# DRAM weight sums for two pairs per transfer and outside attention, factors of the last up pair in two parts, norm between the first up tiles, PSUM pools fixed per MLP

## Chip, cores and metric

One core of one Trainium2 chip. The metric is the device time of one execution in microseconds; the median of three runs of the kernel before is 1159.86 (1158.82 to 1163.74).

## What is computed

One step of a two-layer streaming encoder on 512 prompt frames and 64 sample frames, which the kernel treats together as T = 576 tokens, in halves of HT = 288. Model width 1024, hidden width of the MLP 4096, all in float32.

```python
x = x + pool_mixer(rmsnorm(x))                 # layer 0
x = x + mlp(rmsnorm(x), w_up[0], w_down[0])
x = x + sparse_attention(rmsnorm(x))           # layer 1: indexer scores, top-k, softmax on the chosen keys, w_o
x = x + mlp(rmsnorm(x), w_up[1], w_down[1])
y = rmsnorm(x)

def _mlp(h, w_up, w_down):
    u = jax.nn.relu(h @ w_up)
    return (u * u) @ w_down
```

## The kernel before

**Arithmetic.** Every weight and activation is split in a high and a low part (ACT casts the high part at L206, VectorE or, in the late part of attention, GpSimd subtracts for the low part at L207), and each product is three matmuls: high by high, high by low, low by high. With 128x128 weight blocks and 288 tokens in a matmul, TensorE has 8118 matmuls.

**The MLPs** run in four chunks of 1024 hidden units. A chunk has four up steps `up(c, q)`, each two tiles of 128 hidden units, and four down steps. Three forms of a step exist. A *plain* up step (L558) multiplies tile by tile. A *pair* (`DownPair`, L463, and `UpPair`, L475) is a 2x2 block product with seven multiplications in place of eight (Strassen's scheme in Winograd's form); it needs four sums of weight blocks, s1 to s4, and seven factors of the activations, among them four sums t1 to t4. Layer 0 has plain ups and 16 down pairs; its weight sums are made by GpSimd in SBUF (L267 to L272). Layer 1 has 12 up pairs (chunks 1 to 3), 12 down pairs (chunks 0 to 2), plain ups in chunk 0 and plain downs in chunk 3. The program order is: the ups of chunk c, then the first up of chunk c+1, then the downs of chunk c. The factors of a finished up step (squared ReLU times norm, sums, casts: L578 to L602) are needed by the first down pair of the chunk.

**Layer 1's weight sums are made in DRAM.** For each of the 24 pairs and each of s1 to s4 SyncE issues a copy of one 256 KB block into the DRAM tile `mixed` (L228), and GpSimd issues a DMA that accumulates another block on it (L222, `accum_op=add`). s2 builds on s1, s4 on s2. The generator `mixing()` (L209) yields 56 steps; `next(mixes)` drives it: one step in each up step of layer 0 and each up pair of layer 1, one in each down step, and one in each attention step from u = 18 on (L1358). The copies issued in layer 0's part are 61, in attention 35, in layer 1's MLP none. SyncE loads the finished sums in layer 1 as weights (`raw<-mixed`, L145).

**Queues.** SyncE's instruction stream is a single queue, in order: loads of MLP weights, copies into `mixed`, moves of q (L1282, L1286), cache_k loads (L1087), x from its copy in DRAM (L1397). ScalarE issues loads of w_o and w_in (L145) in its own stream, between its computations. GpSimd's stream holds the accumulates between its arithmetic. An instruction that waits holds all behind it in its stream. The order within a stream is set by a scheduler with a model of time (its table isn't part of the kernel), from the program order.

**PSUM** has eight banks. A phase opens pools (`stage`): at the start of an MLP six banks `po` and two `pf`; at the first pair this phase is closed and opened anew with two `seeds` and six `po` (layer 1), or `seeds`, four `po` and two `pd` (layer 0). The norm's sums and its spread over the partitions (L329 to L341) take banks from `po`, after the first two up tiles.

Of the kernel before, what the change touches and what calls it, by code (L numbers as in the profile page):

```python
# [16 lines left out]
P = 128  # L17
D = 1024
KT = D // P
# [30 lines left out]
def pool_dsa_kernel(ctx: ExitStack, tc: tile.TileContext, a, o):  # L50
# [56 lines left out]
    def f32(t):  # L107
        return t.bitcast(F32)
# [43 lines left out]
    mixed = dram.tile([P, 28, 4, 512], F32, name="mixed")  # L152
    pairs = {}
    for c in range(4):
        for q in range(PLAIN[1][c], 4):
            pairs["up", c, q] = len(pairs)
        if c < 3:
            for q in range(4):
                pairs["down", c, q] = len(pairs)

    def rows(kind, layer, c, q):

# [46 lines left out]

    def mixing():  # L210

        def parts(p):
            kind, c, q = order[p]
            (a11, a12), (a21, a22) = ([r[:, i * 512:(i + 1) * 512] for i in range(2)] for r in rows(kind, 1, c, q))
            s1, s2, s3, s4 = (mixed[:, p, i] for i in range(4))
            return {"s1": (s1, a21, a22), "s3": (s3, a21, a11), "s2": (s2, s1, a11), "s4": (s4, s2, a12)}

        order, copied = list(pairs), []
        for n in range(len(order) + 4):
            for step in (((n, "s1"), (n, "s3")), ((n - 1, "s2"), (n - 2, "s4"))):  # L220
                for dst, add in copied:
                    pool.dma_start(dst, add, accum_op=ALU.add)  # L222
                copied.clear()
                for p, name in step:
                    if 0 <= p < len(order):
                        dst, src, add = parts(p)[name]
                        with tc.issue_after(last_of["sync"].ins):
                            nc.sync.dma_start(dst, src)  # L228
                        copied.append((dst, add))
                yield  # L230

    mixes = mixing()

    def loaded():

        waiting, held = [], 0
        while jobs or waiting:
            while jobs and held < LOADS_AHEAD["more" in phase] and ("last" in phase or jobs[0][0] not in ("pair", "made")):
                kind, *srcs = jobs.pop(0)
                if kind == "made":  # L240
                    r1, r2 = rows(srcs[0], 1, *srcs[1:])
                    m = mixed[:, pairs[tuple(srcs)]].rearrange("p a b -> p (a b)")
                    srcs = [r1, m[:, :1024], m[:, 1024:], r2[:, 512:]]
# [57 lines left out]
    def project(pt, w, xs, between=iter(()), cols=((0, HT), (HT, HT))):  # L301

        n = len(xs)
        for k in range(n):
            next(between, None)
            wh, wl = at(w, k)
            for i, (wt, part) in enumerate(((wh, 0), (wh, 1), (wl, 0))):
                for h, (c, m) in enumerate(cols):
                    pe.matmul(  # L309
                        pt[h][:, :m] if isinstance(pt, tuple) else pt[:, h, :m], wt, xs[k][:, part, c:c + m],  # L310
                        start=(k == 0 and i == 0), stop=(k == n - 1 and i == 2),
                    )

    class Norm:
# [19 lines left out]
        def spread(self):  # L334
            diag = diagonals(self.r)
            self.rb = tmp("rb" + self.s, "rb", 1)
            for h in range(2):
                pb = psum1("rb")
                pe.matmul(pb[:, :HT], ones, diag[:, h * HT:(h + 1) * HT], start=True, stop=True)
                act.copy(self.rb[:, h * HT:(h + 1) * HT], pb[:, :HT])  # L340
            return self.rb  # L341
# [131 lines left out]
            dve.tensor_tensor(d, d, bank[:, :HT], ALU.add)  # L473

    class UpPair(Pair):  # L475
        def __init__(self, us, seeded, v):
            super().__init__(us, seeded, True)
            self.v = v
# [6 lines left out]
        def out(self, i, h, bank):  # L485
            d = self.v[:, 2 * i + h]
            if h:
                act.copy(d, bank[:, :HT])
            else:
                dve.tensor_tensor(d, self.e[:, i], bank[:, :HT], ALU.add)  # L490

    def mlp(layer, gi, strassen, order=range(KT), end=None):
        us = [[None] * KT for _ in range(4)]
# [64 lines left out]

        def up_plain(order):
            w = next_block()  # L560
            pt = [psum1("up", "pf" if "pf" in phase and not turn[0] else "po") for _ in range(2)]
            turn[0] += 1
            for n, k in enumerate(order):
                for i, (part, wt) in enumerate(((0, 0), (1, 0), (0, 1))):
                    for h in range(2):
                        pe.matmul(pt[h][:, :HT], w[:, wt, k * P:(k + 1) * P], moving(k, part, h),  # L566
                                  start=n == 0 and i == 0, stop=n == KT - 1 and i == 2)
            return pt
# [35 lines left out]
        def factors_by_tile(i, v, u):  # L604
# [41 lines left out]
        turn, banks = [0], []  # L646

        def seeded():
            if not banks:
                turn[0] = 0  # L650
                parts.close()
                parts.enter_context(stage(seeds=1, po=6) if layer else stage(seeds=1, pd=2, po=4))
                banks.extend(phase["seeds"].tile([P, 512], F32, tag=f"seed{i}", bufs=1, name=uid("seed")) for i in range(2))
            turn[0] += 1
            if turn[0] <= len(banks):
                pe.matmul(banks[turn[0] - 1][:, :HT], ones, bx0, start=True, stop=True, skip_group_check=True)
            return banks[(turn[0] - 1) % len(banks)]
# [1 line left out]
        bx0 = norm.s2[:, :HT]  # L659

        def up(c, q):
            if not layer or q >= PLAIN[layer][c]:
                next(mixes, None)
            if q >= PLAIN[layer][c]:
                v = new_v()
                pair = UpPair(bx, seeded(), v)
                pair.opening()
                pair.closing()
                activated(v)
                finished(c, q, v)  # L670
                return
            first = (c, q) == (0, 0)
            pts = []
            if not layer and not first and not late:
                v = new_v()
                for i in range(2):
                    pt = up_plain(range(KT))
                    for h in range(2):
                        dve.scalar_tensor_tensor(v[:, 2 * i + h], pt[h][:, :HT], 0.0, halves(norm.rb)[:, h], ALU.max, ALU.mult)
                    act.activation(v[:, 2 * i:2 * i + 2], v[:, 2 * i:2 * i + 2], AF.Square)  # L680
                    if (c, q) == (3, 3):
                        us[c][q] = us[c][q] or u_tile()
                        factors_by_tile(i, v, us[c][q])
                if us[c][q] is None or q == 0:
                    finished(c, q, v)
                return
            for i in range(2):
                pts.append(up_plain(order if first else range(KT)))
                if late:
                    norm.spread()  # L690
                    v = new_v()
                    activated(v, late.pop())
                    finished(c, 0, v)
                if not first:
                    with tc.issue_after(last_of["diag"].ins), tc.issue_after(last_of["rt"].ins):
                        next(mixed, None)
            if first:
                norm.stats()
                late.append(pts)
                return  # L700
            v = new_v()
            activated(v, pts)
            finished(c, q, v)

        late, mixed = [], mixing()
# [324 lines left out]
    def attention(parts):  # L1030
# [302 lines left out]
        def steps():  # L1333

            ranked = {0}
            for u in range(-4, total + 2):
# [178 lines left out]
```

## Time and profile before

| | us |
|---|---|
| median of three runs | 1159.86 |
| profiled execution | 1165.96 |
| its span | 1164.2 |
| pooling mixer | 0 to 43 |
| MLP of layer 0 | 43 to 441 |
| projections of attention and index scores | 441 to 606 |
| late attention (softmax, values, w_o) | 606 to 741 |
| MLP of layer 1 | 741 to 1093 |
| final norm and the last downs | 1093 to 1164 |

The stages' bounds are read from the timeline. In the views, `out<-in` names the tiles that an instruction writes and reads; `idle before <-X` in brackets is the time for which the engine had nothing to do ahead of it and what ended that. PE is TensorE, DVE VectorE, ACT ScalarE, POOL GpSimd, SP SyncE, and a `q` behind an engine's name (SPq, ACTq, POOLq) is its DMA issuing. In a row of the waits the numbers are microseconds in total, times, and the longest.

### The profile page before, as it was taken

To read this page: it belongs to the slowest core of one execution; us is meant where nothing else is said; L and a number is where in the kernel's file an instruction comes from. 1 tells how busy PE (TensorE), PEld (TensorE's weight loads), DVE (VectorE), ACT (ScalarE), POOL (GpSimd) and SP (SyncE) were. 2 spreads that over 40 slices of the span, in tenths; PEclk is the share of its full clock that TensorE was granted. 3 is DMA by queue.
4 is the path that set the end of the run, shared out by engine and by line. 5 is a ranking of instruction groups with operands and counts; after the bars stand their busy time and mean duration, and the time that the engine had idled before them with its cause. 6 is when DMAs were issued, how large, how long until landed. Compare 5 with 4: busy or idle time off the path is not lost.

```text
span 1164.2 us, 20675 instructions
## 1 busy us (share of the span) xinstructions
PE 1104.6 (95%) x8118; PEld 1086.0 (93%) x8118; DVE 808.9 (69%) x1438; ACT 555.6 (48%) x925; POOL 307.4 (26%) x275
## 2 busy tenths in 40 slices
PE   9999999999999989999797897999999999999995
PEld 8999999899999989999787896999999899999995
DVE  7767667666666886479996852568767857865544
ACT  8444343334333454354484554555536636634531
POOL 3023514332532630168874661000000000000002
PEclk9999999999999999999898995999999999999997
DMA  6346686586676674456559995243455555545402
GB/s 215 111 124 163 153 210 149 142 199 163 154 190 165 156 207 148 144 162 177 176 133 236 283 262 133 71 152 96 128 156 161 155 162 154 164 143 175 136 19 82
DMA packets 81746, 183.55 MB, mean 158 GB/s; under 512 B 12289, under 2 KB 23856, under 8 KB 81648
## 3 DMA queue, kind: packets, MB, share of 16 engines
q1 hardware_dynamic: 63072, 139.71, 38.7%
q0 software_dynamic: 13824, 25.17, 14.5%
q10 hardware_dynamic: 4752, 17.34, 4.6%
q8 instruction: 64, 1.05, 0.4%
q14 instruction: 34, 0.28, 0.1%
HBM read 167.10 MB, written 61.22 MB: 196 GB/s over the span
## 4 chain that ended last, share of the span: by engine, by line
PE 53%; DVE 9%; DMA 9%; issue 3%; POOL 3%; ACT 3%; SPq 0%; DVEq 0%; ACTq 0%; POOLq 0%
PE seed L412 13%; PE c L412 8%; PE up L566 8%; PE a L412 8%; PE dn L309 4%; PE pj L309 3%; DVE w L207 2%; DMA mixed<-in_w_down 2%; DMA raw<-in_cache_k 2%; DMA raw<-in_w_down 2%; PE v L1061 1%; ACT w L206 1%; DVE work L1192 1%; DMA mixed<-mixed 1%; DVE m L1191 1%
## 5 line engine op out<-in xcount | busy, mean ns | idle before, releaser
L206 ACT CAST w<-raw 128x1024 fp32r<-128x1024 f32 (+2 forms) x242 | 211.6, 890 | 236.4 <-PE seed L412 85.8
L207 DVE TENSOR_TENSOR w<-raw,w 128x1024 fp32r<-128x1024 f32 (+2 forms) x224 | 244.6, 1098 | 66.2 <-ACT w L206 64.3
L566 PE MATMUL up<-xs,w 128*128 128x288 f32 x1536 | 205.8, 295 | 0.5 <-ACT rbm L340 0.5
L566 PEld LDWEIGHTS up<-xs,w 128*128 128x128 f32 x1536 | 203.8, 188 | 0.9 <-ACT rbm L340 0.9
L412 PE MATMUL seed<-u,w 128*128 128x288 f32 x1008 | 148.6, 297 | 10.1 <-ACT seed L437 4.4
L412 PEld LDWEIGHTS seed<-u,w 128*128 128x128 f32 x1008 | 138.9, 188 | 11.9 <-ACT seed L437 5.3
L757 POOL TENSOR_TENSOR x<-x,spare 128x320 f32<-128x320 f32 (+1 forms) x9 | 8.1, 935 | 434.9 <-ACT spare L753 434.9
L412 PE MATMUL a<-u,w 128*128 128x288 f32 x672 | 104.1, 302 | 2.6 <-ACT w L206 1.7
L412 PE MATMUL c<-u,w 128*128 128x288 f32 x672 | 102.8, 299 | 2.2 <-DVE x L469 0.9
L412 PEld LDWEIGHTS a<-u,w 128*128 128x128 f32 x672 | 96.2, 193 | 3.9 <-ACT w L206 2.2
L412 PEld LDWEIGHTS c<-u,w 128*128 128x128 f32 x672 | 94.9, 191 | 3.3 <-issue 1.1
L309 PE MATMUL pj<-xs,w 128*128 128x288 f32 x672 | 93.0, 294 | 0.0
L309 PEld LDWEIGHTS pj<-xs,w 128*128 128x128 f32 x672 | 90.5, 188 | 0.8
L267 POOL TENSOR_TENSOR sum<-raw 128x512 f32<-128x512 f32 x16 | 24.9, 1556 | 152.7 <-DMA raw<-in_w_down 145.0
L222 POOL DMA_DIRECT2D mixed<-in_w_down x48 | 40.4, 927 | 87.9 <-DMA mixed<-in_w_down 52.8
L207 DVE TENSOR_TENSOR w<-sum,w 128x1024 fp32r<-128x1024 f32 (+1 forms) x32 | 42.0, 1313 | 29.7 <-ACT w L206 29.7
L412 PE MATMUL seed<-bx,w 128*128 128x288 f32 x432 | 62.5, 296 | 0.0
L412 PEld LDWEIGHTS seed<-bx,w 128*128 128x128 f32 x432 | 59.3, 188 | 0.1
L222 POOL DMA_DIRECT2D mixed<-in_w_up x48 | 43.6, 1012 | 40.2 <-DMA mixed<-mixed 21.9
L309 PE MATMUL dn<-u,w 128*128 128x288 f32 (+2 forms) x384 | 52.1, 296 | 1.0 <-ACT u L295 1.0
L309 PEld LDWEIGHTS dn<-u,w 128*128 128x128 f32 x384 | 51.2, 188 | 1.4 <-ACT u L295 1.2
L206 ACT CAST w<-sum 128x1024 fp32r<-128x1024 f32 (+1 forms) x32 | 26.6, 833 | 48.3 <-POOL sum L272 41.1
(279 smaller groups left out, 1993.7 us busy)
## 6 DMA issues: line engine op xcount, KB each, us to landing
raw<-in_w_up SPq DMA_DIRECT2D x52, 512.0 KB, 3.7
raw<-in_w_down SPq DMA_DIRECT2D x52, 512.0 KB, 3.6
raw<-mixed SPq DMA_DIRECT2D x48, 512.0 KB, 3.7
mixed<-in_w_down POOLq DMA_DIRECT2D x48, 256.0 KB, 5.4
mixed<-mixed SPq DMA_DIRECT2D x48, 256.0 KB, 4.9
mixed<-in_w_up POOLq DMA_DIRECT2D x48, 256.0 KB, 5.3
raw<-in_w_o ACTq DMA_DIRECT2D x16, 512.0 KB, 4.5
raw<-in_w_in ACTq DMA_DIRECT2D x15, 512.0 KB, 4.1
```

The source lines that it names most:

```text
L206: act.copy(w[:, 0, at], src[:, at])
L207: how["sub"].tensor_tensor(w[:, 1, at], src[:, at], f32(w[:, 0, at]), ALU.subtract)
L222: pool.dma_start(dst, add, accum_op=ALU.add)
L267: pool.tensor_tensor(s[:, :512], r2[:, :512], r2[:, 512:], ALU.add)
L309: pe.matmul(pt[h][:, :m] if isinstance(pt, tuple) else pt[:, h, :m], wt, xs[k][:, part, c:c + m], start=(k == 0 and i == 0), stop=(k == n ...
L412: pe.matmul(bank[:, :HT], wt[:, at], ut, start=first and j == 0 and i == 0, stop=j == 3 and i == 2, skip_group_check=True)
L566: pe.matmul(pt[h][:, :HT], w[:, wt, k * P:(k + 1) * P], moving(k, part, h), start=n == 0 and i == 0, stop=n == KT - 1 and i == 2)
L757: pool.tensor_tensor(x[k][:, t], x[k][:, t], rb, ALU.mult)
L1061: pe.matmul(pt[:n, :264], xs[k][:, part, i * P:i * P + n], wt, start=(k == 0 and j == 0), stop=(k == KT - 1 and j == 2))
L1191: dve.max(m8[:np_], wk[:np_])
L1192: dve.match_replace(wk[:np_], m8[:np_], wk[:np_], TAKEN)
```

## The change

1. `mixing()` moves two neighbouring pairs per transfer: 48 copies and 48 accumulates of 512 KB in place of 96 and 96 of 256 KB, a new group of two pairs every third step, with s2's copy four steps after s1's and s4's four steps after that. The order of the pairs follows: chunk 0's downs, then for each chunk its ups (0, 1), downs (0, 1), (2, 3), ups (2, 3).
2. `next(mixes)` is gone from attention. In layer 0 it stands after each up tile of q = 1, 2 and in the down steps 1 to 3; in layer 1 after each plain up tile, in each up pair and in the down steps 1 and 3.
3. An up pair with q = 3, where the chunk's downs are pairs (chunks 1 and 2 of layer 1), makes its factors in two parts (`factors_by_part`), the first when three of its four output blocks are in v, the rest after the fourth.
4. In layer 1 the norm's sums are taken between the first and the second up tile and its spread right behind the second, both in the two seed banks. Plain ups of layer 1 are evacuated tile by tile.
5. The PSUM pools stay as they are for a whole MLP: layer 1 six `po` and two `seeds`; layer 0 two `seeds`, four `po` and two `pd`, the last of which take the first up tile.
6. The first plain down tile of layer 1's last chunk takes its hidden blocks in the order 0, 4, 1, 5, 2, 6, 3, 7.

Below, first SyncE's stream late in attention (q, x and cache_k are what attention loads; `x2` means two such in a row), before:

```order
L228 DMA mixed<-in_w_down 128x512 x2
L228 DMA mixed<-mixed 128x512 x2
L1282 DMA q_7263<-q_6010 128x4x128
L228 DMA mixed<-in_w_down 128x512 x2
L228 DMA mixed<-mixed 128x512 x2
L1282 DMA q_7379<-q_6149 128x4x128
L228 DMA mixed<-in_w_up 128x512 x2
L228 DMA mixed<-mixed 128x512
L1397 DMA x_8097<-xd 128x1152
L228 DMA mixed<-mixed 128x512
L1087 DMA raw_7503<-in_cache_k 128x512
```

and at the same place in the changed kernel (its lines: L1332 and L1336 move q, L1445 x, L1137 cache_k; copies would be L240):

```order
L1332 DMA q_6925<-q_5630 128x4x128
L1332 DMA q_7027<-q_5810 128x4x128
L1332 DMA q_7178<-q_5949 128x4x128
L1332 DMA q_7286<-q_6088 128x4x128
L1445 DMA x_7964<-xd 128x1152
L1137 DMA raw_7402<-in_cache_k 128x512
L1336 DMA q_7397<-q_5630 128x2x64 x2
L1445 DMA x_7965<-xd 128x1152
L1137 DMA raw_7519<-in_cache_k 128x512
```

All copies into `mixed` are gone from between q's moves and the loads of x and cache_k.

GpSimd's stream at the same place, up to the first cache_k (L222 accumulates, L207 makes low parts of w_o, L1399 adds attention's output to x), before:

```order
L222 DMA mixed<-in_w_down 128x512 x2
L222 DMA mixed<-in_w_up 128x512 x2
L222 DMA mixed<-in_w_down 128x512 x3
L222 DMA mixed<-in_w_up 128x512
L207 TENSOR_TENSOR w_7030<-raw_7028,w_7030 128x512 x2
L222 DMA mixed<-in_w_down 128x512 x4
L207 TENSOR_TENSOR w_7189<-raw_7187,w_7189 128x512 x2
L222 DMA mixed<-in_w_down 128x512 x4
L207 TENSOR_TENSOR w_7301<-raw_7299,w_7301 128x512
L222 DMA mixed<-in_w_up 128x512
L207 TENSOR_TENSOR w_7301<-raw_7299,w_7301 128x512
```

and in the changed kernel (L1226 adds up index scores, L205 makes low parts, L1447 adds to x, L307 is the low part of cache_k):

```order
L1226 TENSOR_TENSOR work_5261<-work_5261,rl_6584 64x576
L1226 TENSOR_TENSOR work_5261<-work_5261,rl_6618 64x576
L205 TENSOR_TENSOR w_6961<-raw_6959,w_6961 128x512 x2
L205 TENSOR_TENSOR w_7112<-raw_7110,w_7112 128x512 x2
L205 TENSOR_TENSOR w_7216<-raw_7214,w_7216 128x512
L1447 TENSOR_TENSOR x_7964<-x_7964,wo_6855 128x256 x2
L205 TENSOR_TENSOR w_7216<-raw_7214,w_7216 128x512
L307 TENSOR_TENSOR ck_7400<-raw_7402,ck_7400 128x512
```

What was an accumulate between two low parts is gone; the low parts stand one behind the other.

SyncE's stream in the changed kernel's MLP of layer 1, at the end of its plain up tiles, which before held loads (L145) only:

```order
L145 DMA raw_8481<-in_w_up 128x1024
L240 DMA mixed<-mixed 128x2x512
L145 DMA raw_8554<-in_w_up 128x1024
L145 DMA raw_8556<-mixed 128x1024
L145 DMA raw_8558<-mixed 128x1024
L145 DMA raw_8560<-in_w_up 128x512
L240 DMA mixed<-mixed 128x2x512
L240 DMA mixed<-in_w_up 128x2x512 x2
L240 DMA mixed<-mixed 128x2x512 x2
L240 DMA mixed<-in_w_up 128x2x512 x2
L145 DMA raw_8989<-mixed 128x1024
L145 DMA raw_8985<-in_w_down 128x1024
```

Eight of the transfers of 512 KB (L240) stand between the load of the last plain up weights (raw_8481) and the first down weights (raw_8985).

ScalarE's stream at the end of chunk 2's ups in layer 1 (v_10831 is the last up pair's, v_10957 the next chunk's first pair's; L488 takes a product into v, L579 squares, L595 and L601 cast factors), before:

```order
L206 CAST w_11030<-raw_11021 128x1024
L488 COPY v_10957<-a_10958 128x288
L595 CAST u_10948<-v_10831 128x3x288
L206 CAST w_11081<-raw_11023 128x1024
L488 COPY v_10957<-seed_9042 128x288
L206 CAST w_1378_11097<-raw_11025 128x512
L437 ACTIVATE seed_9043<-a_11079 128x288
L579 ACTIVATE v_10957<-v_10957 128x1152
L601 CAST u_10948<-v_10831 128x4x288
```

and in the changed kernel (v_10727 is the last up pair's, v_10861 the next one's; L498 takes a product, L591 squares, L640 casts factors):

```order
L640 CAST u_10728<-v_10727 128x288
L204 CAST w_10985<-raw_10927 128x1024
L498 COPY v_10861<-a_10862 128x288
L640 CAST u_10728<-v_10727 128x3x288
L447 ACTIVATE seed_8323<-a_10983 128x288
L640 CAST u_10728<-v_10727 128x288
L498 COPY v_10861<-seed_8322 128x288
L204 CAST w_1368_11001<-raw_10929 128x512
L204 CAST w_11051<-raw_11043 128x1024
L204 CAST w_11054<-raw_11045 128x1024
L591 ACTIVATE v_10861<-v_10861 128x1152
```

The last cast of the last pair's factors stood behind both products and the square of the next pair, and now stands behind one product.

The core of the diff:

```diff
+        for kind, lo in ([("up", 0)] if c else []) + ([("down", 0), ("down", 2)] if c < 3 else []) + ([("up", 2)] if c else []):
+            for q in (lo, lo + 1):
+                pairs[kind, c, q] = len(pairs)
...
     def mixing():
-        order, copied = list(pairs), []
-        for n in range(len(order) + 4):
...
+        def stages(g):
+            a11, a12, a21, a22 = sources(g)
+            s3, s4, s1, s2 = (mixed[:, 2 * g:2 * g + 2, i] for i in range(4))
+            return ((s1, a21, a22), (s3, a21, a11)), ((s2, s1, a11),), ((s4, s2, a12),)
+
+        groups = len(pairs) // 2
+        for n in range(3 * groups + 9):
+            for stage, late in enumerate((0, 4, 8)):
+                g, due = divmod(n - late - 1, 3)
+                if due == 0 and 0 <= g < groups:
+                    for to, _, add in stages(g)[stage]:
+                        pool.dma_start(to, add, accum_op=ALU.add)
+            for stage, late in enumerate((0, 4, 8)):
+                g, due = divmod(n - late, 3)
+                if due == 0 and 0 <= g < groups:
+                    for to, src, _ in stages(g)[stage]:
                         with tc.issue_after(last_of["sync"].ins):
+                            nc.sync.dma_start(to, src)
+            yield
...
-        def stats(self):
-            pt = psum1("st")
+        def stats(self, bank=None):
+            pt = bank or psum1("st")
...
+                if self.after and i == 0:
+                    self.after()
...
+            pt = [psum1("up", "pd" if "pd" in phase and not ups else "po") for _ in range(2)]
...
+        def lower(u, at, src):
+            act.copy(u[:, at, 0], src)
+            dve.tensor_tensor(u[:, at, 1], src, f32(u[:, at, 0]), ALU.subtract)
+
+        def factors_by_part(v, u, i):
+
+            b12, b11, b22, b21 = (v[:, n] for n in range(4))
+            at = slice(3 * i, 3 + i)
+            rb = halves(norm.rb)
+            for h, n in ((1, (1, 3)), (0, (0, 2))):
+                for m in n:
+                    if m in range(at.start, at.stop):
+                        dve.scalar_tensor_tensor(v[:, m], v[:, m], 0.0, rb[:, h], ALU.max, ALU.mult)
+            act.activation(v[:, at], v[:, at], AF.Square)
+            if i == 0:
+                lower(u, slice(0, 2), v[:, 1:3])
+                dve.tensor_tensor(b11, b11, b12, ALU.subtract)
+                dve.tensor_tensor(b12, b12, b22, ALU.subtract)
+                dve.tensor_tensor(b22, b22, b11, ALU.add)
+                lower(u, slice(3, 6), v[:, 0:3])
+                return
+            lower(u, slice(2, 3), v[:, 3:4])
+            dve.tensor_tensor(b21, b21, b22, ALU.subtract)
+            lower(u, slice(6, 7), v[:, 3:4])
...
         def seeded():
-            if not banks:
-                turn[0] = 0
-                parts.close()
-                parts.enter_context(stage(seeds=1, po=6) if layer else stage(seeds=1, pd=2, po=4))
-                banks.extend(phase["seeds"].tile([P, 512], F32, tag=f"seed{i}", bufs=1, name=uid("seed")) for i in range(2))
...
         def up(c, q):
-            if not layer or q >= PLAIN[layer][c]:
+            if q >= PLAIN[layer][c]:
                 next(mixes, None)
...
+                in_parts = q == 3 and c < strassen
...
+                for i in range(2):
+                    pts.append(up_plain(order))
+                    if i == 1 - layer:
+                        norm.stats(banks[0])
+                late.append(pts)
+                if layer:
+                    spread()
                 return
             for i in range(2):
...
+                evacuated(i, pt)
+                if layer or q in (1, 2):
+                    next(mixes, None)
...
-        parts.enter_context(stage(po=6, pf=2))
+        parts.enter_context(stage(po=6, seeds=1) if layer else stage(seeds=1, po=4, pd=2))
...
-                    next(mixes, None)
+                    if q % 2 if layer else q:
+                        next(mixes, None)
...
-                project(tuple(pt), w, us[c])
+                project(tuple(pt), w, us[c], ks=range(KT) if m else (0, 4, 1, 5, 2, 6, 3, 7))
...
                     next(first_out, None)
-                if u >= 18:
-                    next(mixes, None)
```

More of the change, by code (lines that the diff above doesn't have):

```diff
@@ L210, in mixing, with sources, view @@
     def mixing():
[L212 to L216, printed above, removed]
-        order, copied = list(pairs), []
-        for n in range(len(order) + 4):
[L220 to L226, printed above, removed]
+        def sources(g):
+            kind, c, q = list(pairs)[2 * g]
+            tiles = a["w_up"][1] if kind == "up" else a["w_down"][1, c]
+            first, second, step = (c * 8 + q, 4, 1) if kind == "up" else (2 * q, 1, 2)
+            tile_step = tiles.ap[0][0]
+            def view(k, col):
+                src = tiles[first + k]
+                (row, n), (one, _) = src.ap
+                return bass.AP(src.tensor, src.offset + col, [(row, n), (step * tile_step, 2), (one, 512)])
+            return view(0, 0), view(0, 512), view(second, 0), view(second, 512)
@@ L299, in split, with project @@
             dve.scalar_tensor_tensor(dst[:, 1], src, scale, f32(dst[:, 0]), ALU.mult, ALU.subtract)
-    def project(pt, w, xs, between=iter(()), cols=((0, HT), (HT, HT))):
-        n = len(xs)
-        for k in range(n):
+    def project(pt, w, xs, between=iter(()), cols=((0, HT), (HT, HT)), ks=range(KT)):
+        for k in ks:
             next(between, None)
@@ L310, in project @@
                         pt[h][:, :m] if isinstance(pt, tuple) else pt[:, h, :m], wt, xs[k][:, part, c:c + m],
-                        start=(k == 0 and i == 0), stop=(k == n - 1 and i == 2),
+                        start=(k == ks[0] and i == 0), stop=(k == ks[-1] and i == 2),
                     )
@@ L327, in add, with spread @@
                 dve.tensor_tensor(self.s2, self.s2, sq, ALU.add)
-        def stats(self):
-            pt = psum1("st")
+        def stats(self, bank=None):
+            pt = bank or psum1("st")
             token_sums(pt, self.s2)
             self.r = rms(pt)
-        def spread(self):
+        def spread(self, banks=None):
             diag = diagonals(self.r)
@@ L560, in up_plain @@
             w = next_block()
-            pt = [psum1("up", "pf" if "pf" in phase and not turn[0] else "po") for _ in range(2)]
-            turn[0] += 1
+            pt = [psum1("up", "pd" if "pd" in phase and not ups else "po") for _ in range(2)]
+            ups.append(pt)
             for n, k in enumerate(order):
@@ L672, in up, with evacuated @@
             first = (c, q) == (0, 0)
-            pts = []
-            if not layer and not first and not late:
-                v = new_v()
-                for i in range(2):
[L677 to L685, printed above, removed]
+            def evacuated(i, pt):
+                for h in range(2):
+                    dve.scalar_tensor_tensor(v[:, 2 * i + h], pt[h][:, :HT], 0.0, halves(norm.rb)[:, h], ALU.max, ALU.mult)
+                act.activation(v[:, 2 * i:2 * i + 2], v[:, 2 * i:2 * i + 2], AF.Square)
@@ new lines, in spread @@
+            def spread():
+                nonlocal v
+                norm.spread(banks)
+                v = new_v()
+                for i, pt in enumerate(late.pop()):
+                    evacuated(i, pt)
+                finished(0, 0, v)
+            v = None
+            if first:
+                pts = []
+                for i in range(2):
+                    pts.append(up_plain(order))
[4 more added lines that the diff above has]
+                    spread()
@@ L686, in up @@
                 return
             for i in range(2):
-                pts.append(up_plain(order if first else range(KT)))
+                pt = up_plain(range(KT))
                 if late:
-                    norm.spread()
+                    spread()
+                if not i:
                     v = new_v()
-                    activated(v, late.pop())
-                    finished(c, 0, v)
-                if not first:
+                evacuated(i, pt)
+                if layer or q in (1, 2):
+                    next(mixes, None)
@@ L695, in up @@
+                if layer:
                     with tc.issue_after(last_of["diag"].ins), tc.issue_after(last_of["rt"].ins):
                         next(mixed, None)
[L697 to L705, printed above, removed]
+                if not layer and (c, q) == (3, 3):
+                    us[c][q] = us[c][q] or u_tile()
+                    factors_by_tile(i, v, us[c][q])
@@ L706, in mlp @@
+            if layer or (c, q) != (3, 3):
+                finished(c, q, v)
+        late, mixed, ups = [], mixing(), []
         parts = ExitStack()
-        parts.enter_context(stage(po=6, pf=2))
+        parts.enter_context(stage(po=6, seeds=1) if layer else stage(seeds=1, po=4, pd=2))
+        banks.extend(phase["seeds"].tile([P, 512], F32, tag=f"seed{i}", bufs=1, name=uid("seed")) for i in range(2))
         for c in range(4):
```

24 lines of the change are left out of this document (10 added, 14 removed).

## The prediction

> **What bounds the kernel now.** I read the page first: the span, the clock by slices, the DMA share by slices.
>
> ```profile
> span 1164.2 us, 20675 instructions
> PE 1104.6 (95%) x8118; PEld 1086.0 (93%) x8118; DVE 808.9 (69%) x1438; ACT 555.6 (48%) x925; POOL 307.4 (26%) x275
> PEclk9999999999999999999898995999999999999997
> DMA  6346686586676674456559995243455555545402
> ```
>
> TensorE is busy 95% of the span, so only three things can shorten the kernel: fewer matmuls (the change removes none), idle time of TensorE (59.6 us), and time in which its clock is not full. The clock falls in slices 20, 22 and, most, 25 (698 to 728 us), and the DMA share is at 9 in slices 22 to 24 (611 to 698 us). The windows by stage show which stages are worth work: MLP of layer 0, the last part of attention, MLP of layer 1.
>
> ```profile
> 43.00:441.00 398.00, 387.45 (x2873) 384.53 (x2872) 282.38 (x380) 159.94 (x198) 137.32 (x123) 0.99 0.65 163
> 606.00:741.00 135.00, 117.12 (x826) 111.92 (x826) 71.29 (x204) 63.53 (x158) 57.84 (x62) 0.86 0.83 207
> 741.00:1093.00 352.00, 345.48 (x2540) 342.01 (x2539) 257.96 (x378) 193.03 (x273) 0.00 (x0) 1.00 0.50 149
> ```
>
> (Columns: length; busy time of PE, PEld, DVE, ACT, POOL; granted clock; DMA share; GB/s.) The two MLPs leave TensorE 10.6 and 6.5 us idle at nearly full clock. The 135 us of late attention hold 117.12 us of matmuls at a mean clock of 0.86, about 101 us of work at full clock: **34 us is the most that this stage can give.** Three stalls make nearly all of it:
>
> ```profile
> 620.00:635.00 15.00, 7.33 (x50) 7.03 (x49) 6.49 (x22) 5.25 (x15) 7.33 (x8) 0.77 1.02 245
> 660.00:670.00 10.00, 6.75 (x40) 6.04 (x39) 5.14 (x15) 5.82 (x14) 9.01 (x10) 0.83 1.08 307
> 697.00:705.00 8.00, 3.79 (x30) 3.32 (x28) 0.75 (x1) 1.50 (x4) 3.68 (x5) 0.90 0.99 278
> 705.00:730.00 25.00, 22.49 (x94) 20.78 (x95) 6.88 (x23) 12.38 (x33) 3.44 (x4) 0.50 0.35 82
> ```
>
> The first window holds 7.7 us idle, the second 3.2, the third and fourth 6.7 together; the rest is clock. The waits of these 135 us, by engine, and the timeline around two of the stalls tell what ends last:
>
> ```profile
> POOL mixed L222 <- DMA mixed<-mixed: 25.4, 10, 5.6
> ACT ck L295 <- DMA raw<-in_cache_k: 16.3, 3, 6.0
> PE pt L1248 <- ACT p L1207: 10.9, 3, 7.7
> PE ot L1303 <- DVE wo L1323: 6.5, 1, 6.5
> SPq L228 <- DMA mixed<-in_w_up: 32.8, 8, 8.8
> SPq L228 <- DMA mixed<-in_w_down: 29.9, 8, 6.5
> ...
> 626.63 0.81 POOL L222 DMA_DIRECT2D mixed<-in_w_up  x1 [3.47 <-DMA mixed<-mixed]
> 627.17 2.76 POOL L207 TENSOR_TENSOR w<-raw,w 128x512 fp32r<-128x512 f32 x2
> 629.97 0.34 ACTq L145 DMA_DIRECT2D raw<-in_w_o  x1
> 630.35 0.43 ACT L1310 CAST ot<-ot 128x128 fp32r<-128x128 f32 x2 [8.52 <-POOL w L207]
> 631.44 1.33 PE L1248 MATMUL pt<-ident,p 128*128 128x128 f32 x5 [7.67 <-ACT p L1207]
> ...
> 697.24 0.54 SPq L1087 DMA_DIRECT2D raw<-in_cache_k  x1
> 705.55 0.62 ACT L295 CAST ck<-raw 128x512 fp32r<-128x512 f32 x1 [5.99 <-DMA raw<-in_cache_k]
> 707.51 0.69 PE L1303 MATMUL ot<-ident,on 128*128 128x128 f32 x2 [6.49 <-DVE wo L1323]
> ```
>
> The first is a chain over three in-order engines: POOL stands in an accumulate (L222) until a copy has landed; behind it waits the low half of w_o (L207); until that is made the raw buffer isn't free; ACT stands at the issue of the next w_o load (L145), and the softmax exponential (L1207) behind it is what TensorE needs. The third: a piece of cache_k issued by SP at 697.24 lands at 705.5, after 8.3 us, and ACT's cast (L295) blocks the softmax. The second (660 to 670) is the same cast. In both cases what ends last is a weight sum of layer 1 in DRAM or a load that shares queue or DMA engines with one.
>
> **The change, part by part.**
>
> *No sums in attention.* 35 of the 96 copies and accumulates lie in this stage. Their share of its DMA is seen here:
>
> ```profile
> q0 software_dynamic: 5040, 9.18, 41.3%
> mixed<-mixed SPq DMA_DIRECT2D x19, 256.0 KB, 6.1
> ```
>
> The accumulates are all of queue q0: 41.3% of 135 us, 55.8 us of the 16 engines, 1.6 us each. POOL's and SP's rows in attention are shown with the change: no L222 and no L228 is left, so SP's 62.7 us and POOL's 43.1 us of waits at these lines (the rows above with two smaller ones) have nothing to wait for. Stall 1 (620 to 635): 7.7 us idle, and 3.6 us busy at half clock, some 1.8: 9.5, all removed, since w_o's raw tile was cast by 618.6 and POOL could have gone on 8 us earlier. Stall 2: 3.2 idle and 1.7 of clock; the cache_k load keeps a latency of its own, so I take 4 of 4.9. Stall 3: 6.7 idle, and 22.49 us at clock 0.50 from 705 to 730. The idle part goes: the load lands some 4 us earlier on engines that aren't full, and is issued earlier. Of the slow part at most 11 us can go, but ACT is busy 12.38 of these 25 us and its chain with DVE (softmax, transposes, casts) is serial; at twice the speed TensorE would need 12 us, as long as ACT is busy. I take half, 6. Sum 9.5 + 4 + 6.7 + 6 = **-26**; bounds 0 (DVE or another load ends just as late) and -34.
>
> A rule that speaks to the last 6 us: the Trainium skill ("TensorE: Matmul & The Clock Gate", What's actually happening) says that about 3.4 us of sustained work release the clock. The 25 us of back-to-back matmuls at 0.50 here do not agree with it; by that rule alone this loss would have been 2 us, and the idle time before it is not what holds it.
>
> *The sums that move.* Of the copies, 61 stood ahead of attention and 35 in it (256 KB); now 35 and 13 of 512 KB, so layer 0 carries 70 of the old size and layer 1's MLP 26. At 1.6 us for an accumulate, and about half of that for a copy (the same bytes read once), layer 0 gets 9 x 2.4 = 22 us more of engine time over 398 us: the share goes from 0.65 to 0.70. Layer 1's MLP gets 62 us more over 352: 0.50 becomes 0.68, no more than layer 0 bears already. They are not spread evenly: SP's order has eight copies between the last plain up tiles of its first chunk and the first down weights. Eight copies and accumulates of 512 KB are 8 x 4.8 = 38 us of engine time, where now the share is low:
>
> ```profile
> 741.00:831.00 90.00, 0.00 (x0) 1.00 0.38 119
> ```
>
> 0.38 leaves 56 us free in these 90. Bounds: 0, and +14 if these down weights come that much late; I take **+2**. In layer 0 half as many POOL issues stand in the way of its own sums and of DVE's updates. What they cost now:
>
> ```profile
> PE seed L412 <- DVE x L469: 4.0, 1, 4.0
> PE seed L412 <- ACT seed L437: 2.3, 2, 1.8
> 425.00:430.00 5.00, 4.37 (x22) 0.69 0.98 319
> 210.00:215.00 5.00, 4.62 (x24) 0.68 0.63 214
> ```
>
> Both stalls follow a DVE instruction that ran long while POOL was adding and issuing; with the clock after them they cost some 9 us. A stall like these depends on what happens to coincide; twice the bytes behind one issue can make a new one as easily. Bounds -8 and +6; I take **-2**.
>
> *Factors of the last up pair in two parts* (chunks 1 and 2 of layer 1). Before, the last factors (L601, L602) came behind the next pair's evacuation and square; now behind its first copy only.
>
> ```profile
> PE seed L412 <- ACT seed L437: 2.1, 2, 1.0
> PE a L412 <- ACT w L206: 1.7, 2, 0.8
> PE a L412 <- DVE w L207: 0.7, 2, 0.3
> 925.00:930.00 5.00, 3.67 (x19) 0.86 0.30 77
> 930.00:935.00 5.00, 5.00 (x32) 0.80 0.52 167
> ```
>
> The three waits come once in each of the two chunks, 4.5 us together; the clock after those of chunk 1 costs another 1.5 (3.67 us at 0.86 and 5 at 0.80). More but smaller instructions on ACT and DVE (each part has its own scales, squares and casts) stand beside matmuls: DVE is busy 258 of 352 us. I take **-4** of 6; bounds 0 and -6.
>
> *Norm, PSUM, the last down.* In layer 1 the two waits at the start of the MLP and the one at its last down tile are:
>
> ```profile
> PE up L566 <- ACT rbm L340: 0.9, 1, 0.9
> PE seed L656 <- DVE v L574: 0.5, 1, 0.5
> PE dn L309 <- ACT u L295: 1.0, 1, 1.0
> ```
>
> The norm is made one up tile earlier, and the last down starts with factors that were ready earlier: **-2** of 2.4 (bounds 0, -2.4). In layer 0 four up banks and the two of pd stand in the place of eight, so the third up tile needs a bank whose tile waits for the norm: at worst about two DVE passes, 2.3 us; I take **+1**.
>
> Sum: -26 + 2 - 2 - 4 - 2 + 1 = -31. The profiled execution took 1165.96 us, which gives 1135. It lies 6.1 above the median of 1159.86 (1158.82 to 1163.74). If the executions differ in the stalls that go, the new kernel comes to 1135 whichever is taken; if they differ by something constant, to 1129. I take **1132**.
>
> **Rivals.**
> (A) *A serial chain binds late attention.* From 705 to 730 ACT is busy for half of the time, and cache_k, x and q loads still share SP's queue. If only the 17.6 us of idle time is won for half, and no clock, the stage gives 9 to 14: about 1147. Against it: DVE is busy only 71 of the 135 us, and neither DVE nor ACT is saturated in a stall. 0.13.
> (B) *The MLPs give it back.* The sums cost the same engine time elsewhere. The Trainium skill says so ("DMA: Bandwidth & Descriptors", Issuing engines are not separate DMA queues): all issuers end on the same 16 engines. Here 0.83 of DMA share falls where it hurts, and 0.50 to 0.65 elsewhere did not. With the two upper bounds, +14 and +6, instead of +2 and -2: -31 + 20 = -11, about 1149 to 1155. 0.08.
> (C) *Slower.* The down weights of layer 1's first chunk starve. Eight pairs of 512 KB transfers stand on SP's and POOL's queues ahead of them; free time there is 56 us and need is 38 by the mean cost; an accumulate is ordered behind its copy, and the next copy behind that, so a copy that waits at the head of SP's queue stops every load behind it. In attention such a wait lasted up to 8.8 us (SPq L228 above). Slower begins where four or more of them add over 31 us of idle TensorE: five at 8.8, with the clock after each, give 44 and a time of about 1172. Against it: each dependent copy now comes four steps after its predecessor, not one. 0.04.
> (D) *It doesn't do what it says*, that is, sums still run in attention: excluded by the order of SP and POOL, except for transfers issued late in layer 0 that run on; 0.01, about 1155.
>
> **How the numbers follow.** Forecast 0.74, at 1132, by its own bounds 1118 to 1143 (attention -20 to -34, the rest -14 to +4). The range takes in A and most of B: 1115 to 1151. A measurement of this kernel can tell about 0.5%, 5.8 us, from no change: faster is below 1154, which holds the forecast, A and most of B; same holds a remainder of A, B and D; slower is C. Faster 0.89, same 0.07, slower 0.04.
>
> **What would show it.** In the profile of the changed kernel: no q0 traffic and no wait at the mixed lines between 606 us and the end of attention; a DMA share there below 0.5; the stage about 109 us long, without a PE wait over 3 us; and, for A, a PE wait on softmax or a clock of 0.5 in its last 25 us all the same. In layer 1's MLP a share of 0.65 to 0.7, no PE wait on DMA in its first chunk (B, C: one there), and the two transitions without the waits on ACT's seed and w. In layer 0 no new wait longer than 4 us. The prediction is wrong if late attention stays over 125 us with the sums gone, or if an MLP is longer by more than 10.

## The result, and the profile after

The changed kernel takes 1122.3 us (1120.58 to 1127.65, four executions) beside 1161.8 (1158.82 to 1166.86) of the kernel before, a ratio of 0.9663 (95% interval 0.9614 to 0.9713). The same kernel on another chip gave 1129.73 and a ratio of 0.9723 (0.9661 to 0.9785), where 0.961 to 0.971 had been expected; three of its four executions have a lower clock (last section). The profiled execution took 1127.65. Its page:

```profile
span 1125.9 us, 20515 instructions
PE 1091.3 (97%) x8118; PEld 1073.9 (95%) x8118; DVE 790.7 (70%) x1448; ACT 557.7 (50%) x937; POOL 293.6 (26%) x227
PEclk9999999999999999999999997999999999999997
DMA  6264488389469867457642341458977565555402
```

The matmuls are the same 8118; idle time of TensorE fell from 59.6 to 34.6 us. The DMA share of slices 22 to 24, which was 9, is 2, 3 and 4; new 9s stand in slices 10 and 13, in layer 0's MLP, and in slice 29 (788 to 816 us), early in layer 1's.

To compare equal work, the program is cut where named matmuls start or end. The view of the tiles pj, up and dn gives these rows (first and last start of a group, in us), of before:

```profile
L309 PE MATMUL pj<-xs,w x672: 288/294/402, 442.1 to 563.8; 128*128 128x288 f32 x168
L566 PE MATMUL up<-bx,w x288: 288/295/300, 760.8 to 815.3; 128*128 128x288 f32 x144
L309 PE MATMUL dn<-u,w x384: 274/295/522, 1092.7 to 1148.1; 128*128 128x288 f32 x120, 128*128 128x320 f32 x36, 128*128 128x256 f32 x36
```

and of after:

```profile
L319 PE MATMUL pj<-xs,w x672: 288/294/399, 440.5 to 554.7; 128*128 128x288 f32 x168
L578 PE MATMUL up<-bx,w x288: 288/295/300, 726.2 to 779.0; 128*128 128x288 f32 x144
L319 PE MATMUL dn<-u,w x384: 274/295/522, 1057.9 to 1111.9; 128*128 128x288 f32 x120, 128*128 128x320 f32 x36, 128*128 128x256 f32 x36
```

From the last pj to the first up of layer 1 is attention, and so on; the first pj isn't used as a mark, because in the changed kernel more of the last downs stand ahead of it. The same marks in every kernel of this study give (us):

| kernel | start to end of projections | attention | MLP of layer 1 | last downs and norm | span |
|---|---|---|---|---|---|
| before | 563.8 | 197.0 | 331.9 | 71.5 | 1164.2 |
| after | 554.7 | 171.5 | 331.7 | 68.0 | 1125.9 |
| after, again | 555.0 | 175.7 | 332.1 | 68.0 | 1130.8 |
| e1: before, quiet attention | 566.0 | 165.6 | 331.8 | 71.2 | 1134.6 |
| e2: after, busy attention | 552.9 | 179.3 | 324.3 | 68.7 | 1125.2 |
| e3: one pair each | 565.6 | 165.8 | 338.7 | 69.5 | 1139.6 |
| e4: whole factors | 552.1 | 163.4 | 336.1 | 68.7 | 1120.3 |
| e5: idle copies | 553.5 | 167.7 | 331.0 | 68.6 | 1120.8 |
| e6: all sums in layer 0 | 577.0 | 164.4 | 324.1 | 68.7 | 1134.2 |
| e7: later in layer 1 | 553.6 | 163.5 | 324.9 | 68.0 | 1110.0 |
| e8: no sums | 556.9 | 165.2 | 324.3 | 68.3 | 1114.7 |
| e9: idle sums | 554.2 | 170.0 | 330.1 | 67.9 | 1122.2 |

The kernels ran on several chips, so the text compares stretches within the profiles, and whole times by their ratio to before.

So the 38.3 us of the two spans are 9.1 up to the end of the projections, 25.5 in attention, 0.2 in layer 1's MLP and 3.5 at the end. The second profile of the changed kernel has the first and the last of these again (555.0 and 68.0), so they are not chance. TensorE's longest waits in attention, after:

```profile
PE pt L1298 <- ACT p L1257: 4.6, 2, 4.4
PE sc L1278 <- ACT rp L1159: 1.2, 1, 1.2
PE o L1321 <- DVE on L1346: 1.1, 1, 1.1
```

The waits of 7.7, 2.9 and 6.5 us are gone. TensorE's waits in layer 0's MLP, after:

```profile
PE seed L422 <- ACT seed L447: 1.2, 2, 1.0
PE c L422 <- DVE w L205: 1.2, 2, 0.7
PE seed L422 <- DVE x L479: 0.6, 2, 0.4
```

The waits of 4.0 and 1.8 us are gone. In layer 1's MLP a new stall stands in the place of what was saved (waits, the timeline around it, and the windows on both sides of it):

```profile
PE a L422 <- ACT w L204: 4.5, 4, 2.4
PE a L422 <- DVE w L205: 1.5, 2, 0.7
...
762.95 0.57 SPq L240 DMA_DIRECT2D mixed<-mixed  x1
763.57 1.27 SPq L240 DMA_DIRECT2D mixed<-in_w_up  x2
764.94 1.54 SPq L240 DMA_DIRECT2D mixed<-mixed  x2
766.53 2.12 SPq L240 DMA_DIRECT2D mixed<-in_w_up  x2
...
791.07 1.04 ACT L204 CAST w<-raw 128x1024 fp32r<-128x1024 f32 x1 [5.62 <-DMA raw<-in_w_down]
792.17 0.53 PE L422 MATMUL a<-u,w 128*128 128x288 f32 x2 [2.37 <-ACT w L204]
...
766.00:786.00 20.00, 20.00 (x150) 19.79 (x149) 15.72 (x26) 10.89 (x16) 6.78 (x6) 1.00 1.03 279
786.00:806.00 20.00, 15.30 (x96) 14.14 (x95) 10.99 (x16) 8.29 (x11) 2.25 (x2) 0.91 1.09 274
```

Seven copies leave SP within 6 us, because SP had stood at a load that waited for its buffer; they and their accumulates fill the DMA engines (share 1.03 and 1.09), and the first down weights land late (the clump of the experiments below). The two transitions from ups to downs (chunks 1 and 2), which the prediction priced at 2.2 us of waits each, now show 1.0 each.

### The profile page after: what moved, and what is told of

It is laid out like the page before. It is cut to its first block, busy times and chain, and to the rows that moved or that the text cites. A ratio compares the mean times of both kernels' runs of the same rounds, so it can differ in the third digit from the quotient of the medians.

```text
span 1125.9 us, 20515 instructions
## 1 busy us (share of the span) xinstructions
PE 1091.3 (97%) x8118; PEld 1073.9 (95%) x8118; DVE 790.7 (70%) x1448; ACT 557.7 (50%) x937; POOL 293.6 (26%) x227
## 5 line engine op out<-in xcount | busy, mean ns | idle before, releaser
L205 DVE TENSOR_TENSOR w<-raw,w 128x1024 fp32r<-128x1024 f32 (+2 forms) x224 | 244.6, 1099 | 68.9 <-ACT w L204 68.6
L578 PE MATMUL up<-xs,w 128*128 128x288 f32 x1536 | 205.8, 295 | 0.5 <-DVE v L713 0.5
L578 PEld LDWEIGHTS up<-xs,w 128*128 128x128 f32 x1536 | 203.8, 188 | 0.9 <-DVE v L713 0.9
L422 PE MATMUL a<-u,w 128*128 128x288 f32 x672 | 101.5, 298 | 6.2 <-ACT w L204 4.5
L422 PEld LDWEIGHTS a<-u,w 128*128 128x128 f32 x672 | 93.8, 189 | 8.0 <-ACT w L204 5.4
L234 POOL DMA_DIRECT2D mixed<-in_w_down x24 | 27.6, 1196 | 173.2 <-DMA mixed<-mixed 128.7
L234 POOL DMA_DIRECT2D mixed<-in_w_up x24 | 27.5, 1207 | 140.6 <-DMA mixed<-mixed 121.3
L205 DVE TENSOR_TENSOR w<-sum,w 128x1024 fp32r<-128x1024 f32 (+1 forms) x32 | 33.4, 1044 | 33.1 <-ACT w L204 33.1
L713 DVE SCALAR_TENSOR_TENSOR v<-up,rbm 128x288 f32<-128x288 f32 x80 | 32.5, 450 | 27.2 <-PE up L578 27.1
```

Of the source, the lines that this page charges most:

```text
L205: how["sub"].tensor_tensor(w[:, 1, at], src[:, at], f32(w[:, 0, at]), ALU.subtract)
L234: pool.dma_start(to, add, accum_op=ALU.add)
L422: pe.matmul(bank[:, :HT], wt[:, at], ut, start=first and j == 0 and i == 0, stop=j == 3 and i == 2, skip_group_check=True)
```

## Experiments

Where the text gives no edit of its own, a diff is against the changed kernel.

**e1: only attention is quiet** (against the kernel before).

```diff
-                if u >= 18:
-                    next(mixes, None)
```

> The kernel before, with its step of the weight sums taken out of attention and nothing else changed: the 24 steps that ran there run in the up and down pairs of layer 1's MLP, in transfers of 256 KB. Theory (the sums in attention make the three stalls of late attention): the stretch from the last projection of attention to the first up tile of layer 1 falls from 197 us to 170 to 175, the idle waits of 7.67, 2.88 and 6.49 us go, and the layer 0 MLP stays as in the kernel before (9 us longer than in the changed kernel); the time is 0.975 to 0.983 of before. Rival (the other parts did it, or layer 1 gives the gain back): 0.99 or more, with new TensorE waits in the first chunk of layer 1's MLP.

1133.18 us, 0.9796 (0.9741 to 0.985). Attention takes 165.6 us, 31.4 less and below the 170 to 175 that were expected; the other three stretches stay within 2.2 us. Its longest waits in attention:

```profile
PE pt L1248 <- ACT p L1207: 4.6, 2, 4.4
PE sc L1228 <- ACT rp L1109: 1.2, 1, 1.2
```

The waits of 7.7, 2.9 and 6.5 us are gone (the 4.4 stands at the start of attention in all these kernels). The sums in attention caused the stalls, and layer 1's MLP takes the 24 steps, of 256 KB, at no cost here.

**e2: sums in attention, in the new form** (the two lines added back, with the changed kernel's transfers).

> The changed kernel with a step of the weight sums in each attention step from u = 18 on, as before the change; the transfers stay at 512 KB, and those that ran in layer 1's MLP run in attention now (13 copies and 13 accumulates, 26 of the old size against 35 before). Theory (sums in attention stall it): late attention takes 10 to 25 us longer than in the changed kernel, with waits of ACT or POOL on mixed and cache_k, less some 5 us that the MLP of layer 1 no longer loses at its first down pair; time 0.975 to 0.99 of before. Rival (only the small transfers of before hurt): within 0.5% of the changed kernel, about 0.966.

1129.95 us, 0.9777 (0.9713 to 0.984). Attention takes 179.3 us, 14 to 16 over the kernels in which it is quiet and undisturbed (163.4 to 165.8), and 4 to 8 over the changed kernel's two profiles, so the 10 to 25 that were expected show only against a full clock. Layer 1's MLP falls to 324.3, which gives 7 of it back: in all, e2 is not to be told from the changed kernel (1122.3 and 1129.73). The chain of stall 1 is back:

```profile
625.55 1.14 POOL L234 DMA_DIRECT2D mixed<-in_w_down  x1 [9.32 <-DMA mixed<-mixed]
628.49 2.92 POOL L205 TENSOR_TENSOR w<-raw,w 128x512 fp32r<-128x512 f32 x2
631.82 0.43 ACT L1360 CAST ot<-ot 128x128 fp32r<-128x128 f32 x2 [8.20 <-POOL w L205]
632.83 2.82 PE L1317 MATMUL o<-V,pT 128*128 128x64 f32 x12 [5.35 <-DVE ot L1362]
```

POOL stands for 9.32 us before an accumulate (3.47 in stall 1), and TensorE waits 5.35 us at the end of the chain (7.67 there).

**e5: the same engines loaded, nobody waiting.**

```diff
+                if u >= 18:
+                    with tc.issue_after(last_of["sync"].ins):
+                        for n in range(4):
+                            k = next(asides, None)
+                            if k is not None:
+                                nc.sync.dma_start(aside[:, k], a["w_down"][0, k // 24, k % 8][:, :512])
```

> The changed kernel with 64 copies of 256 KB from DRAM to DRAM added in late attention, on SP's queue, into a tensor that nothing reads, so that no engine waits for them and POOL issues none. They load the DMA engines (some 54 us of them, against some 91 for the sums of before) without blocking POOL. If the stalls come from POOL and ACT standing in their queues behind sums: late attention is less than 4 us longer than in the changed kernel, cache_k lands later (6 us in place of 3) but is hidden. If the load on the DMA engines alone makes them: 10 us or more longer, with ACT waiting for cache_k.

**e9: POOL's accumulates, without a wait** (as e5, two in a step, `pool.dma_start(..., accum_op=ALU.add)`, behind POOL's low parts of w_o).

> The changed kernel with 36 accumulates of 256 KB added in attention, issued by POOL between its low parts of w_o, into a tensor that nothing reads and with no copy ahead of them; as many as stood in attention before, and none waits for anything. If what stalled the kernel before was POOL waiting in front of them: late attention (from the last projection to layer 1's first up tile) stays at 163 to 176 us as in the quiet kernels. If POOL's issuing itself or the load that accumulates put on the DMA engines (some 58 us here) does it: 10 us or more over that, with ACT or TensorE waiting for POOL's w or for cache_k.

e5 took 1122.53 us, e9 1124.87; attention 167.7 and 170.0 us. In e5 cache_k's loads land later (median 5.2 us against 2.9), and TensorE's waits for the softmax grow from 4.6 to 6.8 us. A window from the middle of attention, of e5 and then of e9:

```profile
610.00:670.00 60.00, 57.77 (x475) 55.52 (x475) 45.58 (x124) 38.32 (x87) 22.41 (x20) 1.00 0.99 329
```

```profile
640.00:674.00 34.00, 34.00 (x287) 33.20 (x286) 20.97 (x57) 21.76 (x48) 26.02 (x30) 1.00 0.98 231
```

At a DMA share of 0.98 to 0.99, as in the stalls before, TensorE is busy for 96% and 100% of the time at full clock. The load on the DMA engines (e5), and as many POOL issues as before (e9), cost 2 to 7 us by the quiet kernels. Each of the two carries about three fifths of the load of the sums (54 and 58 us against 91, by the estimates above), at the same share; both at once were not run. What they lack is the waits, so the waits in the in-order queues made most of the 31.

**e3: the same places, 256 KB each.**

```diff
...
-                        pool.dma_start(to, add, accum_op=ALU.add)
+                        for j in range(2):
+                            pool.dma_start(to[j], add[j], accum_op=ALU.add)
...
-                            nc.sync.dma_start(to, src)
+                            for j in range(2):
+                                nc.sync.dma_start(to[j], src[j])
```

> The changed kernel with each transfer of 512 KB cut into two of 256 KB, issued one behind the other at the same place: 96 copies and 96 accumulates as before the change, the same bytes, the same places. Theory A (in layer 0 it is the number of POOL's DMA issues that stretches VectorE's and POOL's work): layer 0's MLP gets back 4 to 9 us of its gain, with a wait on a slow VectorE instruction of over 1.5 us. Theory B (it is where the transfers stand, or chance): layer 0 within 2 us, the whole within 0.5% of the changed kernel.

1138.18 us, 0.9799 (0.9742 to 0.9857), where the changed kernel on the same chip has 0.9723. Up to the projections' end it takes 565.6 us, like before (563.8) and e1 (566.0), and unlike all kernels with 512 KB transfers at these places (552.1 to 555.0). The stall of before at 425.63 us,

```profile
416.97 6.29 DVE L327 TENSOR_TENSOR s<-s,sq 128x576 f32<-128x576 f32 x1
425.63 2.21 PE L412 MATMUL seed<-u,w 128*128 128x288 f32 x12 [4.04 <-DVE x L469]
```

is back, at the same place of the program:

```profile
419.28 0.81 POOL L233 DMA_DIRECT2D mixed<-in_w_up  x1
419.85 1.56 POOL L279 TENSOR_TENSOR sum<-sum,raw 128x512 f32<-128x512 f32 x1
419.88 6.32 DVE L337 TENSOR_TENSOR s<-s,sq 128x576 f32<-128x576 f32 x1
421.10 1.54 POOL L281 TENSOR_TENSOR raw<-raw,raw 128x512 f32<-128x512 f32 x1
422.34 1.92 POOL L233 DMA_DIRECT2D mixed<-in_w_up  x2
423.43 2.14 POOL L283 TENSOR_TENSOR sum<-sum,raw 128x512 f32<-128x512 f32 x1
428.58 2.74 PE L422 MATMUL seed<-u,w 128*128 128x288 f32 x10 [3.20 <-DVE x L479]
```

A VectorE addition that takes 0.74 us elsewhere, and 1.83 us at this place of the changed kernel, runs 6.32 us while POOL adds and issues without a gap; the adding of a product to x (L479) behind it is late, and TensorE waits. Theory A holds against theory B. The edit doubles SP's copies too; that POOL's issues are the half that matters is read from these rows, and no run doubles one without the other. In layer 1 the cut transfers cost another 7 us (338.7).

**e4: whole factors** (`in_parts = False`).

> The changed kernel with the factors of the last up pair of chunks 1 and 2 made whole, as before the change. Theory: the waits at those two transitions grow from 1.0 to about 2.2 us each, with some clock behind them; 3 to 5 us longer than the changed kernel, 0.969 to 0.971 of before. Rival (the waits are set by weights, not by factors): no longer by more than 1 us.

1124.63 us, 0.9699 (0.9645 to 0.9753): not to be told from the changed kernel by time, since attention differs by 8 to 12 us between these profiles for a reason that is no part of the edit (see the last section). Layer 1's MLP takes 336.1, 4.0 to 4.4 more than the changed kernel's. At the two transitions it waits 4.8 us in all, against 2.0; among these is a wait that the changed kernel's MLP of layer 1 doesn't have:

```profile
PE seed L422 <- ACT seed L447: 2.1, 2, 1.0
```

The other 1.2 to 1.6 us are not shown to come from the factors: over the 60 us around the first down pairs the clock is 0.94, against 0.97 in the changed kernel.

**e7: later in layer 1.**

```diff
-                if layer or q in (1, 2):
+                if not layer and q in (1, 2):
                     next(mixes, None)
...
-                    if q % 2 if layer else q:
+                    if layer or q:
                         next(mixes, None)
```

> The changed kernel with the steps of the sums in layer 1 moved: none after its plain up tiles, one in every down step in place of every second; so the eight transfers that stood in a clump ahead of the first down weights are spread over the pairs. Theory (the clump makes the 4.7 us of waits at the first down pairs of layer 1, at a DMA share of 1.1): those waits go, 4 to 6 us less than the changed kernel, 0.961 to 0.963 of before. Rival (the sums then come late, or each pair's weights do): same time or longer, with waits on raw<-mixed later in that MLP.

1112.09 us (1110.16 to 1113.62), 0.9584 (0.9537 to 0.9631): better than both kernels. Layer 1's MLP takes 324.9 us, 6.8 to 7.2 less than in the changed kernel. The rest of the distance is attention at full clock (163.5 us against 171.5 and 175.7), of which the edit isn't shown to be the cause. The longest waits in that MLP, and a stretch of 60 us:

```profile
PE a L422 <- ACT w L204: 1.2, 2, 0.6
PE c L422 <- ACT w L204: 0.8, 2, 0.4
...
797.00:857.00 60.00, 60.00 (x452) 60.00 (x452) 41.74 (x57) 31.00 (x43) 6.77 (x6) 1.00 0.99 280
```

In these 60 us, at a share of 0.99, TensorE has no idle time. The longest waits that are left are those of the two transitions; those at the first down pairs are gone.

**e6: all sums in layer 0** (`if not layer:` in the first place of e7's diff, the second as it was).

> The changed kernel with a step of the sums after each plain up tile of layer 0 (all q), so that all 48 copies and accumulates run in layer 0 and none in layer 1. Theory (the clump in layer 1 costs 7 us and layer 0 has room): the MLP of layer 1 takes 324 to 325 us as without sums, layer 0 stays within 2 us, 1110 to 1114 us in all, like the kernel with later steps. Rival (layer 0's DMA engines, at a share of 0.7 with 70 of the old transfers, fill up with 96): layer 0 loses 4 us or more in waits on weights or on the sums made by POOL.

1138.46 us, 0.9833 (0.9776 to 0.9889). Layer 1 takes 324.1, but layer 0 loses 22 us. Its waits in layer 0's MLP, and the timeline at the third:

```profile
PE seed L422 <- ACT seed L447: 12.7, 3, 5.0
...
311.69 2.31 POOL L234 DMA_DIRECT2D mixed<-in_w_up  x2
313.11 3.22 POOL L234 DMA_DIRECT2D mixed<-in_w_down  x2
314.51 3.11 POOL L283 TENSOR_TENSOR sum<-sum,raw 128x512 f32<-128x512 f32 x1
317.65 0.62 ACT L204 CAST w<-sum 128x512 fp32r<-128x512 f32 x1 [9.33 <-POOL sum L283]
320.79 1.57 PE L422 MATMUL seed<-u,w 128*128 128x288 f32 x5 [5.04 <-ACT seed L447]
```

The rival was right, and POOL is where it shows: it issues four accumulates ahead of the last part of one of its own weight sums, ACT waits 9.33 us for that, and the evacuation that TensorE needs is behind ACT's cast. The fuller DMA engines (a share of 0.93 from 172 to 308 us) have a part that no run separates: POOL's first addition, which waits for a load, starts 6.8 us ahead of the pair's first product, against 8.9 in the changed kernel.

**e8: no sums.** `groups = 0`, and the pairs load plain weights in their place: the sums of layer 1's weights are left out.

> The changed kernel without any copy or accumulate of weight sums: layer 1's pairs take plain weights in the place of the sums, so its output isn't the reference's; matmuls, loads and casts keep their number and size. It shows what the sums still cost after the change. Theory: 5 us less in the MLP of layer 1 (the waits at its first down pairs go), 0 to 2 us in layer 0, 0 in attention: 1115 to 1118 us by the changed kernel's 1122. Rival (the sums still cost much in layer 0, by POOL standing in the way of VectorE): 10 us or more less, most of it there.

1116.06 us, 0.9646 (0.9568 to 0.9724). Layer 1's MLP takes 324.3 us, 7.4 less than the changed kernel's; up to the end of the projections it is 2 us longer than with sums, so the rival is out and nothing is left to gain there. e7 with all its sums is within 0.6 us of it, or shorter, in every stretch.

## Why the prediction was right, and where it was off

1132 was predicted, in 1115 to 1151; the two medians lie 10 and 2 below it. That the sum came so near is partly luck: layer 0 and the end of the kernel gave some 10 us more than forecast, and the sums in layer 1's MLP took 5 more. The forecast's own bounds of 1118 to 1143 are narrower than its terms: they take -48 from 1166 and -16 from 1160. By its steps:

- *No sums in attention, -26.* Right in mechanism: e1 shows it alone (31.4), e5 and e9 that waiting in queues, not load, was the main cause. The 25.5 of the profile agree with the sum by luck: the last term, 6 of 11 us for the slow clock, was a mean between two outcomes. The clock is either full there (attention 163.4 to 165.8, nearly all of the 34 us) or half again for a time (171.5, 175.7).
- *Layer 0, -2 and +1.* Mis-sized: -9.1 up to the end of the projections. The stalls had been priced at "some 9 us", but as a coincidence that could come back; e1 and e3 show that the 4 us one comes back (4.3 and 3.2) with small accumulates at these places, and it is gone in all kernels with those of 512 KB there. The bound of -8 was also passed. The new wait for a PSUM bank is 0.5 us (PE up L578, behind DVE v L713).
- *The sums in layer 1's MLP, +2.* Mis-sized: about 7 (e2, e7 and e8 take 6.8 to 7.4 less). The place was named, the eight transfers ahead of the first down weights, but the free time was counted over 90 us, while SP let seven of them go within 6.
- *Factors in two parts, -4.* Right: the waits fell from 4.5 to 2.0 us, and the 1.5 of slow clock behind those of chunk 1 is gone (1.00 in the changed kernel). In e4 the waits alone come back, 2.8.
- *Norm and last down, -2.* The three waits are gone from the profile. The end of the kernel gained 3.5 us, of which this explains 1.0 and a shorter wait of the last norm (PE st, from 1.2 to 0.5) another 0.7; the cause of the rest stays open.
- Rival A's slow clock is seen in some executions; B and C's clump is real at 7 of the 31 us that C needs. D is out: queue q0 moves nothing in late attention.

## What to carry to other kernels

A transfer that nobody needs soon still costs when an engine stands in its queue waiting for it: in attention a share of 0.98 to 0.99 of the DMA engines cost 2 to 7 us (e5, e9), and the sums, with waits ahead of needed work, 31 (e1). When background transfers are moved, look at the instructions that stand behind them in each in-order queue, and at where a blocked queue will let several go at once; spreading 13 of them differently was worth another 7 us. Fewer, larger transfers can matter for the engine that issues them: with the same bytes in transfers of half the size, layer 0 took 11 us more (e3).

## What was not expected of the hardware

TensorE's clock can fall with almost no idle time. After, late in attention (windows of TensorE alone), and then e7 at the same place, whose program is the same up to there:

```profile
679.00:684.00 5.00, 4.81 (x27) 0.70 0.37 108
684.00:689.00 5.00, 5.00 (x22) 0.50 0.00 0
689.00:694.00 5.00, 5.00 (x23) 0.50 0.00 2
694.00:699.00 5.00, 5.00 (x37) 0.94 0.00 0
```

```profile
681.00:686.00 5.00, 5.00 (x41) 1.00 0.00 2
686.00:691.00 5.00, 5.00 (x37) 1.00 0.00 0
```

The longest wait just ahead of it was 1.14 us (for VectorE), against 0.2 at most in e7, and the half clock lasts some 13.6 us (by these windows) of small matmuls with no idle time between them. The Trainium skill ("TensorE: Matmul & The Clock Gate", What's actually happening) lets the clock fall after an idle window of about 3.4 us and rise after as long a busy one; neither agrees with these rows. The eight executions of the changed kernel form two groups, 1120.3 to 1122.5 us with a granted clock of 0.986 to 0.988 over the whole and 1127.7 to 1132.5 with 0.980 to 0.983; the two that were profiled are of the second. What decides it, and why e7's four executions all had the full clock (0.991 to 0.992), stays open.
